# The low halves of the weights: from a subtraction on VectorE or GpSimd to a negating copy on ScalarE and an adding transfer

## The chip, the cores and the metric

The kernel runs on one core of a Trainium2 chip. The metric is the device time of one execution in microseconds (us). The kernel before takes 1946.34 us (median of 3 runs, 1944.94 to 1948.01).

The core has a matrix engine (TensorE: PE for the matmuls, PEld for the loads of their stationary operand), three engines for elementwise work (VectorE: DVE; ScalarE: ACT; GpSimd: POOL) and a queue for loads and stores (SyncE: SP). Each engine works through its own instructions in order; an instruction that waits for a semaphore holds up all behind it on that engine. Transfers can be issued from SP, ACT and POOL.

## The reference

One layer of a streaming encoder, applied to 1024 + 32 rows of width 1024, all in float32:

- an input layer norm;
- `x = LN1(alpha*x + 1/2*g1*SwiGLU_1(mod1(x)))`, with `SwiGLU(h) = (silu(h @ w1) * (h @ w3)) @ w2` and an inner width of 2816;
- `x = LN2(alpha*x + g2 * W_out[RG-LRU ; spatial gating](mod2(x)))`, a mixing stage with a recurrent and a gated branch of width 512 each;
- `x = LN3(alpha*x + 1/2*g3*SwiGLU_2(mod3(x)))`.

`mod_k(x) = x*(1 + scale_k(c)) + shift_k(c)` and `g_k = 1 + gate_k(c)`, where the nine vectors of length 1024 are `silu(c) @ w_ada + b_ada`, for two conditions c (one for the 1024 rows, one for the 32).

## The kernel before

**Precision.** TensorE works on `float32r`, a rounded float32. Each float32 operand is therefore kept as two parts, the rounded value `h` and the remainder `l = x - h`, and each product is three matmuls: `Wh*Xh + Wh*Xl + Wl*Xh`. `split` (L208) makes the parts: ACT copies the source into `h` (L209), and DVE, or another engine that is named, subtracts `h` from the source into `l` (L210).

**Weights.** All weights of the two feed-forward stages and of the mixing stage come as 156 raw tiles of 128x1024 float32 (512 KB), loaded by SP in a fixed order into 5 buffers (`w_raw`, L204). They are used as 440 halves of 128x512. `w_split` (L248) makes the next half of that order: it takes a tile from a ring of 8 buffers (tag `wh`; 12 halves have another home, `wx` or `tx`), finds its source (`w_source`, L229) and splits it. `w_get` (L261) hands a half to the matmuls; `w_rel` (L269) is called when a half has been used, splits as many further halves as the ring then has room for, and loads raw tiles ahead.

**Which engine subtracts.** `w_split` sends the subtraction to POOL where an engine is given, in the "window" around LN1 (`self.window`), and for the halves S1 to S4; otherwise to DVE. Six halves in `ffn_first` are given POOL by name.

**The fast tiles.** From column tile 9 of the first feed-forward stage on, and 3 of the second (32 tiles in all), w1 and w3 of a tile are treated as a 2x2 block matrix with a product of seven multiplications for two of the three row chunks. Such a tile has eight halves: A11, A21, A22, S2, A12, S1, S3, S4. The S halves are sums that POOL forms in place in the raw tiles: A21 -= A11 (L239), then A22 -= A21 (L241), which gives S2, then A11 += A22 (L243) for S1 and A12 -= A22 (L245) for S4; S3 is the changed A21. An in-place sum has to wait until everything that reads the raw tile has read it. `H_fast` (L852) multiplies them in the order A11, A21, S2, A12, S1, S3, A22, S4 and calls `w_rel` after each. `F` (L1006) then multiplies the gated result `g` by w2, for blocks of mostly two tiles; it uses four halves for two tiles.

**Beside it.** In the first feed-forward stage DVE also computes seven of the nine conditioning vectors (`ada_rest`, L685): 56 raw tiles `araw` (L693), in the same 5 buffers as the weights, are multiplied and summed (L759, L761); 14 times the sums go through TensorE to a row (L710), from POOL's queue to DRAM (L711) and back, turned (L716, two transfers), and are used by DVE (L721). POOL also forms block sums of x there (L818, L819) and, in the norms, an inverse square root (L562).

**What sets the order.** TensorE's instructions run in the order of the program. For the other engines a planner orders them: it goes by program order and priorities, and by when it reckons each instruction ready, from modelled durations. `startup` and `ffn_first` are the exception: there ACT, DVE and POOL keep the order that is written. Tile by tile the framework puts in all semaphore waits, a wait for a transfer's landing included.

Of the kernel before, what the change touches and what calls it, by code (L numbers as in the profile page):

```python
# [12 lines left out]
F32 = mybir.dt.float32  # L13
F32R = mybir.dt.float32r
AF = mybir.ActivationFunctionType
ALU = mybir.AluOpType
# [90 lines left out]
def raws_of(e):  # L107

    nm, t, h = e
    return [(nm, t)] if h in (0, 1) else [(f"{nm}w1", t), (f"{nm}w3", t)]  # L110
# [13 lines left out]
class Core:  # L124
# [123 lines left out]
    def w_split(self, e=None):  # L248
        n = self.n_split
        if n >= len(self.order):  # L250
            return
        it = self.order[n]
        e = e or (self.nc.gpsimd if self.window or str(it[2])[0] == "S" else None)
        while not all(r in self.raws for r in raws_of(it)):
            self.w_raw()
        w = self.w_tile(it)
        self.split(w[:, 0, :], w[:, 1, :], self.w_source(it), e)
        self.ws[it] = w
        self.n_split += 1

# [114 lines left out]
    def startup(self):  # L375
        nc, V, S = self.nc, self.nc.vector, self.nc.scalar
        sp, es = self.pool("start", side="right")
        self.ada_hl = []
        self.n_ada = 0
        self.ada_rw = []  # L380
        xt = []
        for i in range(9):
            if i < 8:
                t = sp.tile([P, D], F32, name=f"xt{i}")
                for h in range(2 if i == 0 else 1):
                    cs = slice(h * 512, (h + 1) * 512) if i == 0 else slice(0, D)
                    nc.sync.dma_start(t[:, cs], self.i["x"][i * P:i * P + P, cs])
            else:
                t = self.apool.tile([P, 4, 384], F32, tag="t4", name="xt8", bufs=2).rearrange("p a b -> p (a b)")[:, 0:D]
                nc.sync.dma_start(t[:NS], self.i["x"][NP:T])  # L390
            xt.append(t)

        self.nat = 4
        self.ada_nat = []
        for f in range(self.nat):
            w = [self.wpool.tile([P, 1024], F32, tag="wh", name="wnat", bufs=RING) for _ in range(2)]
            for j in range(2):
                nc.sync.dma_start(w[j], self.i["ada0"][2 * f + j].rearrange("p k c -> p (k c)"))
            self.ada_nat.append(w)
            if f == min(1, self.nat - 1):  # L400
                self.w_raw()
                self.w_raw()
        self.n_ada = 2 * self.nat
        self.ada_rw = [None] * self.n_ada
        self.ada_hl = [None] * self.n_ada

        for v in range(2):
            S.activation(self.cs[:, :, v], self.v("c", v * 8, v * 8 + 8), AF.Silu)
        self.split(self.c4[:, :, 0:2], self.c4[:, :, 2:4], self.cs)
        mv = sp.tile([P, 9, 2], F32, name="mv")  # L410
        rs = sp.tile([P, 9, 2], F32, name="rs")

        def stats(i):
            n = P if i < 8 else NS
            bs = sp.tile([P, 2, 6], F32, tag="bs", name="bs", bufs=2)
            for h in range(2):
                V.bn_stats(bs[:n, h, :], xt[i][:n, h * 512:(h + 1) * 512])
            V.bn_aggr(mv[:n, i, :], bs[:n])
            self.rsqrt(rs[:n, i, 0:1], mv[:n, i, 1:2])

        def norm(i):
            n = P if i < 8 else NS
            if i in (5, 8):
                V.tensor_scalar(xt[i][:n], xt[i][:n], mv[:n, i, 0:1], rs[:n, i, 0:1], ALU.subtract, ALU.mult)
                return
            V.scalar_tensor_tensor(rs[:n, i, 1:2], mv[:n, i, 0:1], -1.0, rs[:n, i, 0:1], ALU.mult, ALU.mult)
            S.activation(xt[i][:n], xt[i][:n], AF.Identity, scale=rs[:n, i, 0:1], bias=rs[:n, i, 1:2])

        banks = {}

        def turn(i):

            m = P if i < 8 else NS
            banks[i] = [self.ps() for _ in range(2)]
            for k in range(K):
                o = (k % 4) * P
                nc.tensor.transpose(banks[i][k // 4][:, o:o + m], xt[i][:m, k * P:(k + 1) * P], self.idn[:m, :m])
                self.pe += 0.213

        def out(i, dve):  # L440
            c, j = divmod(i, 3)
            m = P if i < 8 else NS
            for h in range(2):
                d = self.xacc[c][:, 4 * h:4 * h + 4, j * P:j * P + m]
                r = banks[i][h].rearrange("p (k t) -> p k t", k=4)[:, :, :m]
                if dve:
                    V.tensor_copy(d, r)
                else:
                    S.activation(d, r, AF.Copy)

        self.rows = {}
        for i in range(11):
            if i < 9:
                stats(i)
            if 0 < i < 10:
                norm(i - 1)
                turn(i - 1)
            if i == 9:
                self.ada_mm(0)
            if i > 1:  # L460
                out(i - 2, i > 7)
        for h in range(2):
            self.w_split()
        es.close()

    def ada_raw(self, n):
# [1156 lines left out]
```

## Time and profile before

| | before |
|---|---|
| median of 3 runs | 1946.34 us (1944.94 to 1948.01) |
| profiled execution: time | 1944.43 us |
| profiled execution: span of the instructions | 1942.7 us |
| granted TensorE clock, mean | 0.983 |
| PE / DVE / ACT / POOL busy | 1870.9 / 1291.3 / 696.4 / 483.2 us |
| transfers issued from POOL's queue | 42, none above 4 KB |

"Busy" counts the instructions that compute. A row of a list of groups reads: line, engine, operation, what it writes and reads, shape, count, then total busy us and mean ns of one, then the idle time of the engine before them and what ended most of it. A row of a table of stages reads: from and to in us, length, then for each engine the busy time and in brackets the number of instructions, then the granted clock, the busy share of the 16 transfer engines and the rate. A row of a timeline reads: start, duration, engine, line, operation, and in brackets how long the engine idled before it and which instruction released it.

The stages: start and first conditioning to 85 us; first feed-forward stage to about 820 us, with `ada_rest` beside it until about 608 us; LN1, mixing and LN2 to about 1215 us; the second feed-forward stage to about 1882 us; then the last norm.

### The profile page before, as it was taken

How to read it: one execution, taken by the hardware profiler on the slowest of the kernel's cores; microseconds unless marked ns; L12 is line 12 of the kernel's file. 1: busy time of each engine (PE TensorE's matmuls, PEld its weight loads, DVE VectorE, ACT ScalarE, POOL GpSimd, SP SyncE). 2: the span in 40 equal slices, each digit the busy share in tenths (PEclk: the TensorE clock that was granted, in tenths of full speed). 3: DMA queues.
4: the chain of work that ended last, by engine and by line, in shares of the span. 5: the costliest groups of instructions: out<-in, count | busy, mean ns of one | idle time of the engine just before them, and what ended most of it. 6: DMA issues, size and time to landing. Idle time of an engine off the chain costs nothing.

```text
span 1942.7 us, 28443 instructions
## 1 busy us (share of the span) xinstructions
PE 1870.9 (96%) x11434; PEld 1820.6 (94%) x11434; DVE 1291.3 (66%) x2296; ACT 696.4 (36%) x1228; POOL 483.2 (25%) x398
## 2 busy tenths in 40 slices
PE   6999999989998999989999999999999999999996
PEld 3899999889898999989979999999999999999996
DVE  7855678898877645683776558875545554555477
ACT  5552122232332232336553517522332233223324
POOL 2201160234333333222000000042334233323410
PEclk9999999999998999989989999999999999999998
DMA  7332333132331111122011311102120111011102
GB/s 275 125 115 77 110 103 121 59 104 93 98 127 37 44 66 44 55 87 93 28 33 51 133 55 44 44 23 65 45 65 22 58 53 64 24 53 57 44 1 90
DMA packets 40500, 140.16 MB, mean 72 GB/s; under 512 B 5652, under 2 KB 8340, under 8 KB 39600
## 3 DMA queue, kind: packets, MB, share of 16 engines
q1 hardware_dynamic: 37104, 128.98, 19.6%
q10 hardware_dynamic: 1920, 9.24, 1.2%
q0 software_dynamic: 1344, 0.12, 0.4%
q8 instruction: 90, 1.47, 0.3%
q14 instruction: 42, 0.34, 0.1%
HBM read 129.53 MB, written 8.79 MB: 71 GB/s over the span
## 4 chain that ended last, share of the span: by engine, by line
PE 81%; DVE 10%; ACT 3%; issue 2%; DMA 2%; POOL 2%; SPq 0%; POOLq 0%; DVEq 0%; ACTq 0%
PE ps L152 78%; DVE acc L761 1%; PE psl L152 1%; DVE xl L548 1%; DVE wh L210 1%; DMA mod<-mrow 1%; PE psa L152 1%; PE psz L152 1%; PE psm L152 1%; DMA araw<-ada 1%; DVE s L674 0%; PE psg L152 0%; ACT t L538 0%; POOL s L818 0%; DVE tot L980 0%
## 5 line engine op out<-in xcount | busy, mean ns | idle before, releaser
L152 PE MATMUL ps<-xh,wh 128*128 128x384 f32 (+1 forms) x4016 | 953.7, 320 | 6.9 <-ACT s L874 5.0
L152 PEld LDWEIGHTS ps<-xh,wh 128*128 128x128 f32 x4016 | 698.9, 189 | 12.2 <-ACT s L874 5.7
L152 PE MATMUL ps<-xl,wh 128*128 128x384 f32 (+1 forms) x2008 | 641.7, 320 | 3.3 <-DVE xl L548 3.2
L152 PE MATMUL ps<-g,wh 128*128 128x384 f32 (+1 forms) x2808 | 474.8, 328 | 17.0 <-DVE s L674 7.1
L152 PEld LDWEIGHTS ps<-g,wh 128*128 128x128 f32 x2808 | 461.3, 191 | 26.8 <-DVE s L674 8.4
L209 ACT ACTIVATE wh<-raw 128x512 fp32r<-128x512 f32 x428 | 266.2, 628 | 524.9 <-PE ps L152 436.8
L152 PEld LDWEIGHTS ps<-xl,wh 128*128 128x128 f32 x2008 | 378.6, 189 | 7.1 <-DVE xl L548 5.3
L210 DVE TENSOR_TENSOR wh<-raw,wh 128x512 fp32r<-128x512 f32 x283 | 204.6, 729 | 246.0 <-ACT wh L209 244.6
L210 POOL TENSOR_TENSOR wh<-raw,wh 128x512 fp32r<-128x512 f32 x145 | 208.8, 1442 | 321.8 <-ACT wh L209 321.5
L974 DVE SCALAR_TENSOR_TENSOR xb<-ps,gt,xb 128x384 f32<-128x384 f32 (+1 forms) x352 | 151.9, 486 | 87.4 <-PE ps L152 71.1
L761 DVE SCALAR_TENSOR_TENSOR acc<-araw,cs,acc 128x512 f32<-128x512 f32 x196 | 154.1, 825 | 15.3 <-DMA araw<-ada 15.1
L152 PE MATMUL ps<-tx,wh 128*128 128x384 f32 x768 | 138.9, 336 | 0.1
L974 DVE SCALAR_TENSOR_TENSOR xa<-ps,gt,xa 128x384 f32<-128x384 f32 (+2 forms) x288 | 122.7, 483 | 22.8 <-PE ps L152 22.8
L152 PEld LDWEIGHTS ps<-tx,wh 128*128 128x128 f32 x768 | 132.5, 188 | 0.6 <-DVE s L867 0.4
L239 POOL TENSOR_TENSOR raw<-raw 128x512 f32<-128x512 f32 x32 | 46.3, 1448 | 324.0 <-DVE wh L210 324.0
L209 ACT ACTIVATE g<-s 128x384 fp32r<-128x384 f32 (+1 forms) x126 | 60.7, 492 | 138.7 <-DVE s L674 138.7
L210 DVE TENSOR_TENSOR g<-s,g 128x384 fp32r<-128x384 f32 (+1 forms) x126 | 84.9, 683 | 23.6 <-ACT g L209 22.5
L867 DVE TENSOR_TENSOR s<-s,ps 128x384 f32<-128x384 f32 x128 | 70.5, 551 | 37.4 <-PE ps L152 37.3
L562 POOL TENSOR_TENSOR r<-r,half 128x3 f32<-128x3 f32 x8 | 7.4, 923 | 310.2 <-DVE r L561 310.2
L669 ACT ACTIVATE s<-ps 128x384 f32<-128x384 f32 (+1 forms) x100 | 44.9, 452 | 99.4 <-PE ps L152 99.1
L152 PE MATMUL ps<-T,wh 128*128 128x384 f32 x384 | 72.9, 337 | 0.0
L152 PEld LDWEIGHTS ps<-T,wh 128*128 128x128 f32 x384 | 67.9, 188 | 0.4 <-issue 0.2
(237 smaller groups left out, 1694.6 us busy)
## 6 DMA issues: line engine op xcount, KB each, us to landing
raw<-wst SPq DMA_DIRECT2D x156, 512.0 KB, 3.3
araw<-ada SPq DMA_DIRECT2D x56, 512.0 KB, 3.3
wnat<-ada SPq DMA_DIRECT2D x8, 512.0 KB, 9.9
raw<-ada SPq DMA_DIRECT2D x8, 512.0 KB, 3.7
xt<-x SPq DMA_DIRECT2D x7, 512.0 KB, 7.7
sp<-xa ACTq DMA_DIRECT2D x2, 1536.0 KB, 5.8
xb<-sp ACTq DMA_DIRECT2D x2, 1536.0 KB, 9.4
y<-xb SPq DMA_DIRECT2D x4, 768.0 KB, 3.3
```

Source lines behind the costliest of these rows:

```text
L152: self.nc.tensor.matmul(out, a, b, start=start, stop=stop, skip_group_check=True)
L209: self.nc.scalar.activation(dst_h, src, AF.Copy)
L210: (e or self.nc.vector).tensor_tensor(dst_l, src, dst_h.bitcast(F32), ALU.subtract)
L239: G.tensor_tensor(a["A21"], a["A11"], a["A21"], ALU.subtract)
L548: V.tensor_tensor(xl, tmp, xh.bitcast(F32), ALU.subtract)
L562: self.nc.gpsimd.tensor_tensor(out, out, self.half[:n, :w], ALU.pow)
L669: self.nc.scalar.activation(s, x[:, :n], AF.Silu)
L761: V.scalar_tensor_tensor(acc[:, v, :], r[:, kk, :], self.cs[:, k, v:v + 1], acc[:, v, :], ALU.mult, ALU.add)
L867: V.tensor_tensor(out, x, ps[:, :n], ALU.add)
L974: V.scalar_tensor_tensor(X[:, m, a + o:a + o + w], ps[:, o:o + w], self.gt[:, s, m, v:v + 1], X[:, m, a + o:a + o + w], ALU.mult, ALU.add)
```

## The change

`w_split` splits a half in the old way only where an engine is given or in the window. Every other half is made so: ACT copies the source into the first part, ACT copies that first part with a factor of -1 into the second part, and a transfer issued from POOL's queue adds the raw source to the second part. The S halves take this way too; before, POOL subtracted them. The two halves at the end of `startup`, which had no engine given and so went to DVE, are now given DVE by name.

```diff
@@ -250,11 +250,18 @@
         if n >= len(self.order):
             return
         it = self.order[n]
-        e = e or (self.nc.gpsimd if self.window or str(it[2])[0] == "S" else None)
+        e = e or (self.nc.gpsimd if self.window else None)
         while not all(r in self.raws for r in raws_of(it)):
             self.w_raw()
         w = self.w_tile(it)
-        self.split(w[:, 0, :], w[:, 1, :], self.w_source(it), e)
+        src = self.w_source(it)
+        if e:
+            self.split(w[:, 0, :], w[:, 1, :], src, e)
+        else:
+
+            self.nc.scalar.activation(w[:, 0, :], src, AF.Copy)
+            self.nc.scalar.activation(w[:, 1, :], w[:, 0, :].bitcast(F32), AF.Copy, scale=-1.0)
+            self.nc.gpsimd.dma_start(w[:, 1, :], src, accum_op=ALU.add)
         self.ws[it] = w
         self.n_split += 1
 
@@ -460,7 +467,7 @@
             if i > 1:
                 out(i - 2, i > 7)
         for h in range(2):
-            self.w_split()
+            self.w_split(V)
         es.close()
```

## The prediction

> **What bounds the kernel now.** I read the page's first block and the groups of line 209 and 210, then the stages, then who waits for whom in the first feed-forward stage.
>
> ```profile
> span 1942.7 us, 28443 instructions
> ...
> PE 1870.9 (96%) x11434; PEld 1820.6 (94%) x11434; DVE 1291.3 (66%) x2296; ACT 696.4 (36%) x1228; POOL 483.2 (25%) x398
> ...
> L209 ACT ACTIVATE wh<-raw 128x512 fp32r<-128x512 f32 x428 | 266.2, 628 | 524.9 <-PE ps L152 436.8
> ...
> L210 DVE TENSOR_TENSOR wh<-raw,wh 128x512 fp32r<-128x512 f32 x283 | 204.6, 729 | 246.0 <-ACT wh L209 244.6
> L210 POOL TENSOR_TENSOR wh<-raw,wh 128x512 fp32r<-128x512 f32 x145 | 208.8, 1442 | 321.8 <-ACT wh L209 321.5
> ```
>
> TensorE is busy 96% of the span. The 428 copies of L209 mostly wait for TensorE to give a ring buffer back, so the weights run as far ahead as the ring allows. The stages say where TensorE is not full:
>
> ```profile
> core 0: us, PE busy (x) PEld busy (x) DVE busy (x) ACT busy (x) POOL busy (x), PEclk, DMA share, GB/s
> 85.00:370.00 285.00, 279.09 (x1699) 272.47 (x1697) 195.14 (x334) 82.25 (x158) 58.67 (x57) 0.99 0.32 104
> 370.00:608.00 238.00, 222.24 (x1313) 214.17 (x1314) 207.91 (x351) 71.54 (x135) 82.60 (x68) 0.96 0.29 94
> 608.00:820.00 212.00, 212.00 (x1316) 212.00 (x1316) 124.39 (x244) 63.40 (x120) 73.60 (x56) 1.00 0.16 53
> 820.00:1058.00 238.00, 225.94 (x1284) 210.09 (x1284) 161.45 (x273) 117.56 (x189) 29.55 (x34) 0.96 0.17 60
> 1058.00:1215.00 157.00, 157.00 (x973) 155.77 (x972) 102.81 (x153) 78.43 (x114) 2.56 (x3) 1.00 0.21 72
> 1215.00:1882.00 667.00, 667.00 (x4176) 666.87 (x4174) 389.29 (x716) 212.28 (x403) 209.48 (x152) 1.00 0.14 45
> ```
>
> From 608 to 820 and from 1058 to 1882 us (1036 us together) TensorE never idles: nothing done to the weights can gain there, it can only lose. TensorE idles 285.00 - 279.09 = 5.9 us from 85 to 370, 15.8 us from 370 to 608 and 12.1 us in LN1 and the mixing. In the second of these DVE is busy 207.91 of 238 us (87%), against 68% in the first. Who waits there (85 to 608 us):
>
> ```profile
> PEld ps L152 <- DVE s L674: 8.4, 4, 3.3
> PEld ps L152 <- ACT g L209: 5.8, 4, 2.2
> ...
> DVE wh L210 <- ACT wh L209: 31.7, 18, 5.1
> DVE mod L721 <- DMA mod<-mrow: 25.9, 8, 4.6
> ...
> DVE acc L761 <- DMA araw<-ada: 15.1, 9, 3.4
> ```
>
> TensorE waits for the gating that DVE has not come to (L674) and for what follows from it, and DVE in turn sits 31.7 us in front of subtractions whose first part isn't there yet.
>
> **The change part by part.** *How many.* There are 440 halves: 428 of tile wh, 12 with another home. The old way stays for 2 in startup, 6 with POOL by name, and 13 of the window (of POOL's 145, 128 are the four S halves of 32 tiles and 6 are named; that leaves 11, and 2 in the other home). So 440 - 2 - 6 - 13 = 419 take the new way; of these POOL subtracted 128 and DVE 291.
>
> *DVE* loses 291 x 0.729 = 212 us. What of it lies where TensorE waits:
>
> ```profile
> 85.00:370.00 285.00, 274.56 (x1669) 270.37 (x1667) 34.72 (x46) 28.97 (x47) 1.13 (x1) 0.99 0.32 104
> 370.00:608.00 238.00, 218.15 (x1287) 212.18 (x1288) 30.13 (x37) 38.41 (x62) 35.77 (x26) 0.96 0.29 94
> ...
> 1215.00:1882.00 667.00, 653.54 (x4090) 652.84 (x4088) 82.18 (x119) 122.48 (x195) 108.65 (x76) 1.00 0.14 45
> ```
>
> These are the same stages for the instructions on weight tiles alone, with L209 and L210 on DVE, ACT and POOL. From 370 to 608 us DVE sheds 30.1 us and falls from 87% to 75%. Between the two stages the idle share of TensorE goes with DVE's: 2.1% (5.9 of 285) at 68%, 6.6% (15.8 of 238) at 87%, a slope of 0.24 points a point. At 75% that is 3.6%, or 8.5 us, a gain of some 7 us. From 85 to 370 DVE falls to 56%, for which the line gives no idling; I take half of the 5.9 us, 3 us. Bounds: no gain, and all 21.7 us plus what the clock of 0.96 and 0.99 costs (0.04 x 238 + 0.01 x 285 = 12 us).
>
> *ACT* gets 419 x 0.628 = 263 us more, 36% to about 50%. In the full stages that is at most 195 x 0.628 = 122 us on top of 212 in 667 us. In the written order at the end of `ffn_first` the last negating copy stands before the first gating:
>
> ```profile
> 84.63 0.63 ACT L209 ACTIVATE wh<-raw 128x512 fp32r<-128x512 f32 x1 [1.34 <-PE ps L152]
> 85.17 0.47 ACT L669 ACTIVATE s<-ps 128x384 f32<-128x384 f32 x1
> ```
>
> The first row, the last of those copies, follows a wait for TensorE that takes up what came before, so only its own second copy is exposed: 0.6 us of loss.
>
> *POOL* sheds 128 x 1.44 = 184 us and gets 419 transfers. A POOL transfer of this shape is not in the trace. The nearest:
>
> ```profile
> L711 POOL DMA_DIRECT2D mrow<-row x14: 534/544/716, 128.8 to 609.2; - x14
> L716 POOL DMA_DIRECT2D mod<-mrow x28: 747/760/814, 131.1 to 614.3; - x28
> ...
> raw<-wst SPq DMA_DIRECT2D x156, 512.0 KB, 3.3
> ...
> xb<-sp ACTq DMA_DIRECT2D x2, 1536.0 KB, 9.4
> ...
> mod<-mrow POOLq DMA_DIRECT2D x28, 2.0 KB, 2.9
> ...
> mrow<-row POOLq DMA_DIRECT2D x14, 4.0 KB, 1.6
> ```
>
> Issuing costs POOL 0.54 to 0.76 us; I take 0.76, 318 us in all, which it has idle. Landing: 1.6 us at the least, 9.4 at the most. The transfer moves 256 KB, half of a raw load, but must read its destination too, so I take the raw load's 3.3 us. The Trainium skill, "DMA: Bandwidth & Descriptors", section on the anatomy of one DMA, gives about 2.0 us plus the bytes at 436 GB/s, an estimate of 2.6 us for 256 KB; its rules for authors add that an accumulate reads its destination and writes it later. For a raw load its formula gives 3.2 us, and this trace has 3.3. With 2.6 the lateness of 4.0 us that follows, and with it the second rival's price, would be 3.3 us.
>
> *Is a half still there in time?* A part that came 0.73 us after the first copy now comes after 0.63 + 0.76 + 3.3 = 4.7 us: 4.0 us later. The longest chain is that of S2, which needs the whole of A22 first, since the in-place sum may not overwrite a raw tile that a transfer still reads:
>
> ```profile
> 1362.01 0.63 ACT L209 ACTIVATE wh<-raw 128x512 fp32r<-128x512 f32 x1 [1.46 <-PE ps L152]
> ...
> 1363.58 1.29 POOL L241 TENSOR_TENSOR raw<-raw 128x512 f32<-128x512 f32 x1 [0.94 <-DVE wh L210]
> ...
> 1365.92 0.63 ACT L209 ACTIVATE wh<-raw 128x512 fp32r<-128x512 f32 x1
> ...
> 1380.88 0.63 ACT L209 ACTIVATE wh<-raw 128x512 fp32r<-128x512 f32 x1 [0.97 <-PE ps L152]
> ```
>
> The first row is A22's copy, the third S2's; the fourth is released by the end of A21's matmuls in the next tile, which is where S2's begin. New: 1362.01 + 1.26 + 0.76 + 3.3 = 1367.3, sum to 1368.6, two copies to 1369.9, transfer to 1373.9. TensorE needs it at 1380.9, so 6.9 us are left, and a landing may take 3.3 + 6.9/2 = 6.8 us before TensorE waits. In the ring as a whole a half has some eight halves of matmuls between its turn and its use. Hence no loss in the full stages. If the cover went, each microsecond of landing above 6.8 would cost 2 us a tile, 64 us in all.
>
> *Raw tiles* come free later by the same 4.0 us. That delays loads of `araw`, for which DVE waits; this I enter with 2 us of loss, between none and the rival below.
>
> *Sum.* 1944.43 - 7 - 3 + 0.6 + 2 = 1937 us, made against the profiled execution's own time (its span of 1942.7 us and 1.7 us around it). The median of the runs is 1.9 us above that time, so the sum stands for some 1939 us of a run; I take **1938 us**, -0.4%, since the clock's part is left out of the sum. A difference of 0.2% (3.9 us) is about what a measurement of this kernel can tell from no change.
>
> **The rivals.**
>
> *ScalarE's line (slower).* At the end of a block of tiles the planner put S2's copy ahead of the silu that the last gating needs (L916), although the copy waits for POOL's sum:
>
> ```profile
> 1331.01 1.37 POOL L241 TENSOR_TENSOR raw<-raw 128x512 f32<-128x512 f32 x1 [2.37 <-DVE wh L210]
> 1331.20 5.96 PE L152 MATMUL ps<-g,wh 128*128 128x384 f32 x36
> ...
> 1332.42 0.63 ACT L209 ACTIVATE wh<-raw 128x512 fp32r<-128x512 f32 x1 [1.95 <-POOL raw L241]
> ...
> 1332.96 0.51 ACT L916 ACTIVATE s<-s 128x384 f32<-128x384 f32 x1
> ...
> 1334.77 0.97 DVE L210 TENSOR_TENSOR g<-s,g 128x384 fp32r<-128x384 f32 x1 [0.59 <-ACT g L209]
> ```
>
> The low part of g ends at 1335.74, and TensorE wants it with the last 6 of the 36 matmuls, about 1336.1: 0.4 us to spare. If the order stays, the sum comes 4.0 us later and the second copy 0.6 after it, so that TensorE waits 4.2 us. With 15 such block ends that is 63 us less the forecast's gain: about 2002 us. For it: the order that is there now. Against it: a planner that reckons with a transfer in the chain sees S2 ready after the silu and puts it behind. It decides at about 0.4 us of lateness.
>
> *Late conditioning (slower).* SP's loads of `araw` wait for weight tiles:
>
> ```profile
> SPq L693 <- DVE wh L210: 83.2, 18, 11.8
> ```
>
> Each of the 18 comes 4.0 us later, up to 72 us of waiting in DVE's line, and POOL's transfers L711 and L716 stand behind weight transfers that wait for ACT. If half of it reaches TensorE, 36 us against the 10 gained: about 1972 us. Against it: DVE sheds 65 us of work there and 31.7 us of waits.
>
> *No change.* TensorE's stalls before 608 us come from the returns of the conditioning rows (25.9 us of DVE waiting at L721) and not from DVE's load; then the relief buys nothing: 1946 us.
>
> *POOL held by its transfers (slower).* A second transfer of L716 starts 3.8 us after the first, with POOL idle between:
>
> ```profile
> 131.06 0.81 POOL L716 DMA_DIRECT2D mod<-mrow  x1 [1.51 <-DMA mrow<-row]
> 134.86 0.76 POOL L716 DMA_DIRECT2D mod<-mrow  x1 [2.99 <-issue]
> ```
>
> If every weight transfer held POOL that long, 195 halves from 1215 to 1882 us would take 741 us beside 101 us of POOL's other work, in 667 us: 175 us of loss there, some 235 in all, about 2180 us. Against it: L716 moves single elements, 128 x 4 runs of 4 bytes, where a weight transfer has 128 runs of 2 KB.
>
> *It doesn't do what it says:* the subtraction could stay where it was only if an engine were given everywhere, which the diff excludes.
>
> **How the numbers follow.** Forecast 0.45, no change 0.20, late conditioning 0.17, ScalarE's line 0.12, POOL held 0.06. The forecast's own range is 1928 to 1942 us. The range for 8 times in 10 leaves out ScalarE's line and POOL held (0.18) and reaches from 1925, where most of the 21.7 us is won, to 1990. Of the forecast 0.43 lies beyond 0.2%. Faster 0.43, same 0.22, slower 0.35.
>
> **What would show it.** Right: 419 transfers of 256 KB on POOL's queue, landing in under 6.8 us; from 608 to 820 and 1058 to 1882 TensorE still full; DVE some 30 us less busy from 370 to 608, and TensorE idle 9 us there and not 16. Wrong: TensorE waiting at the start of w2 blocks for g (ScalarE's line); longer waits of DVE for `araw` or at L721; POOL idle "issue" time before weight transfers; a landing far above 3.3 us, which would break the cover of S2 and with it the forecast.

## The result, and the profile after

The changed kernel takes 1995.31 us (median of 4 runs, 1992.95 to 1998.74) against 1945.64 us of the kernel before beside it: a ratio of 1.0258 (95% interval 1.0236 to 1.028), 2.6% slower. The forecast was 1938 us, with a range of 1925 to 1990 us: the wrong direction, and the time lies outside the range. The profiled execution took 1998.74 us, with a mean granted clock of 0.975 (before 0.983).

First the page after: its first rows, then groups of the halves and their transfers.

```profile
span 1997.0 us, 29461 instructions
...
PE 1883.0 (94%) x11434; PEld 1830.1 (92%) x11434; DVE 1046.6 (52%) x2005; ACT 935.3 (47%) x1647; POOL 659.7 (33%) x689
...
L264 POOL DMA_DIRECT2D wh<-raw x409 | 358.7, 887 | 682.0 <-ACT wh L263 364.3
...
L262 ACT ACTIVATE wh<-raw 128x512 fp32r<-128x512 f32 x409 | 254.1, 625 | 470.2 <-PE ps L152 254.5
...
L263 ACT ACTIVATE wh<-wh 128x512 fp32r<-128x512 f32 x409 | 255.8, 629 | 10.0
...
L239 POOL TENSOR_TENSOR raw<-raw 128x512 f32<-128x512 f32 x32 | 43.4, 1358 | 144.7 <-DMA wh<-raw 117.9
```

(Lines behind `w_split` stand 7 lower now: L669 became L676, and so on.) The change does what it says: 409 of 419 halves are of tile wh, ACT makes both copies in 0.63 us each, and the transfer's issue costs POOL 0.887 us. DVE sheds 244.7 us (1291.3 to 1046.6): the 212 us of the subtractions, and the rest because other work of it ran shorter, such as the low parts of `g` (126 of them took 84.9 us before and 67.6 after; why isn't shown). TensorE's idle time grows all the same, from 71.8 to 114.0 us, and its busy time by 12.1 us for the same 11434 matmuls, with a mean granted clock of 0.975 in place of 0.983. The table of stages, first in stretches that the prediction used, then in two of the second feed-forward stage:

```profile
85.00:370.00 285.00, 274.82 (x1664) 269.75 (x1665) 154.00 (x273) 104.13 (x196) 91.07 (x100) 0.98 0.56 147
370.00:608.00 238.00, 207.04 (x1194) 198.60 (x1194) 155.22 (x291) 97.61 (x178) 92.17 (x94) 0.92 0.59 138
608.00:820.00 212.00, 201.75 (x1240) 199.95 (x1239) 87.28 (x208) 97.30 (x176) 91.00 (x93) 0.98 0.61 131
820.00:1058.00 238.00, 220.90 (x1248) 208.51 (x1247) 142.93 (x239) 121.68 (x203) 52.68 (x59) 0.96 0.33 89
...
1263.00:1880.00 617.00, 617.00 (x3877) 617.00 (x3877) 262.74 (x554) 300.97 (x555) 250.23 (x253) 1.00 0.59 124
1880.00:1935.00 55.00, 51.13 (x293) 50.26 (x292) 20.72 (x39) 24.93 (x48) 20.57 (x22) 0.97 0.54 104
```

From 370 to 608 us DVE is busy 155.22 of 238 us (65%, before 87%), and TensorE idles 31.0 us in place of 15.8, at a clock of 0.92 in place of 0.96. The second feed-forward stage is full, as before, but for its end, which comes some 50 us later than before: from 1880 to 1935 us TensorE idles 3.9 us. Most of the loss lies in the first stage: LN1's first inverse root, on POOL, comes 48.0 us later. Of these, some 10 us are there by 378 us of the time before (a row's copy, L710 before and L717 after, matched one by one), 43 by 593 us (the silu of L916, now L923); then nothing is added until 806 us, and the last 5 at the stage's end. The loss is made from 378 to 600 us above all, where the fast tiles run beside the conditioning. The lateness stays at 48 us up to 1843 us of the time before, and is 54 us from 1859 on. The inverse root's row in the timeline before (L562), then after (L569):

```profile
834.17 1.12 POOL L562 TENSOR_TENSOR r<-r,half 128x3 f32<-128x3 f32 x1 [41.34 <-DVE r L561]
```

```profile
882.20 1.13 POOL L569 TENSOR_TENSOR r<-r,half 128x3 f32<-128x3 f32 x1
```

Who waits for whom from 85 to 860 us, before and then after (sum in us, times, longest):

```profile
POOL raw L239 <- DVE wh L210: 115.3, 13, 14.6
...
DVE mod L721 <- DMA mod<-mrow: 29.1, 9, 4.6
...
ACT wh L209 <- POOL raw L241: 15.2, 8, 3.0
DVE acc L761 <- DMA araw<-ada: 15.1, 9, 3.4
```

```profile
DVE acc L768 <- DMA araw<-ada: 59.3, 15, 9.1
ACT wh L262 <- POOL raw L241: 59.1, 11, 9.5
DVE mod L728 <- DMA mod<-mrow: 51.8, 13, 10.7
...
POOL raw L239 <- DMA wh<-raw: 45.2, 11, 7.0
```

Four waits go with it. POOL's in-place sums (L239) stand until a transfer has read the raw tile; S2's copy on ACT stands behind the sum of L241; DVE waits for the conditioning's raw tiles (four times as long as before) and for its returning rows. POOL idled in front of L239 before as well, and longer, for VectorE's subtractions (115.3 us): that wait alone proves nothing, and what counts is that the sum now comes so late that ACT waits for it, 59.1 us in place of 15.2. One such chain, from the timelines of POOL, ACT, DVE and PE after:

```profile
461.55 1.29 POOL L239 TENSOR_TENSOR raw<-raw 128x512 f32<-128x512 f32 x1 [6.12 <-DMA wh<-raw]
...
466.10 1.25 POOL L241 TENSOR_TENSOR raw<-raw 128x512 f32<-128x512 f32 x1 [2.46 <-DMA wh<-raw]
...
467.39 0.63 ACT L262 ACTIVATE wh<-raw 128x512 fp32r<-128x512 f32 x1 [5.69 <-POOL raw L241]
467.92 0.61 ACT L209 ACTIVATE acchl<-acc 128x512 fp32r<-128x512 f32 x1
...
468.57 0.69 DVE L210 TENSOR_TENSOR acchl<-acc,acchl 128x512 fp32r<-128x512 f32 x1 [5.32 <-ACT acchl L209]
469.18 0.61 DVE L981 SCALAR_TENSOR_TENSOR xa<-ps,gt,xa 128x384 f32<-128x384 f32 x1
...
469.85 1.33 PE L152 MATMUL ps<-g,wh 128*128 128x384 f32 x3 [3.69 <-DVE xa L981]
```

The sum of L239 waits 6.12 us for a transfer, that of L241 2.46 us for the next one; ACT stands 5.69 us; behind its copy stands the copy of `acchl`, DVE waits for that, its gated sum L981, which gives a PSUM buffer back, comes late, and TensorE idles 3.69 us. TensorE waited for no weight here: everything in this chain is work that stood behind a weight in an engine's line.

The 6 us at the end of the second stage have such a chain too, from one timeline of all engines:

```profile
1896.88 1.28 POOL L239 TENSOR_TENSOR raw<-raw 128x512 f32<-128x512 f32 x1 [5.24 <-DMA wh<-raw]
...
1899.53 0.63 ACT L262 ACTIVATE wh<-raw 128x512 fp32r<-128x512 f32 x1 [8.32 <-POOL raw L241]
...
1900.73 0.47 ACT L904 ACTIVATE s<-ps 128x384 f32<-128x384 f32 x1
...
1901.25 0.44 PE L152 MATMUL ps<-xh,wh 128*128 128x384 f32 x1 [2.62 <-ACT s L904]
```

ACT stands 8.32 us in front of S2's copy, the silu of L904 comes behind both copies, and TensorE waits 2.62 us for that silu.

### The profile page after: what moved, and what is told of

Its sections match the earlier page's. It is cut to its first block, busy times and chain, and to the rows that moved or that the text cites. A ratio compares the mean times of both kernels' runs of the same rounds, so it can differ in the third digit from the quotient of the medians.

```text
span 1997.0 us, 29461 instructions
## 1 busy us (share of the span) xinstructions
PE 1883.0 (94%) x11434; PEld 1830.1 (92%) x11434; DVE 1046.6 (52%) x2005; ACT 935.3 (47%) x1647; POOL 659.7 (33%) x689
## 3 DMA queue, kind: packets, MB, share of 16 engines
q0 software_dynamic: 61680, 109.98, 31.3%
## 5 line engine op out<-in xcount | busy, mean ns | idle before, releaser
L264 POOL DMA_DIRECT2D wh<-raw x409 | 358.7, 887 | 682.0 <-ACT wh L263 364.3
L262 ACT ACTIVATE wh<-raw 128x512 fp32r<-128x512 f32 x409 | 254.1, 625 | 470.2 <-PE ps L152 254.5
L263 ACT ACTIVATE wh<-wh 128x512 fp32r<-128x512 f32 x409 | 255.8, 629 | 10.0
L981 DVE SCALAR_TENSOR_TENSOR xb<-ps,gt,xb 128x384 f32<-128x384 f32 (+1 forms) x352 | 152.8, 488 | 119.8 <-PE ps L152 98.4
L768 DVE SCALAR_TENSOR_TENSOR acc<-araw,cs,acc 128x512 f32<-128x512 f32 x196 | 147.5, 800 | 59.3 <-DMA araw<-ada 59.3
L152 PE MATMUL ps<-tx,wh 128*128 128x384 f32 x768 | 144.9, 345 | 18.0 <-DVE s L874 18.0
L152 PEld LDWEIGHTS ps<-tx,wh 128*128 128x128 f32 x768 | 137.4, 194 | 19.1 <-DVE s L874 19.0
L981 DVE SCALAR_TENSOR_TENSOR xa<-ps,gt,xa 128x384 f32<-128x384 f32 (+2 forms) x288 | 123.5, 486 | 37.2 <-PE ps L152 36.6
L239 POOL TENSOR_TENSOR raw<-raw 128x512 f32<-128x512 f32 x32 | 43.4, 1358 | 144.7 <-DMA wh<-raw 117.9
L210 DVE TENSOR_TENSOR g<-s,g 128x384 fp32r<-128x384 f32 (+1 forms) x126 | 67.6, 542 | 36.4 <-ACT g L209 35.4
L676 ACT ACTIVATE s<-ps 128x384 f32<-128x384 f32 (+1 forms) x100 | 44.0, 450 | 71.2 <-PE ps L152 70.9
L681 DVE TENSOR_TENSOR s<-s 128x384 f32<-128x384 f32 x64 | 35.8, 560 | 59.1 <-ACT s L923 58.1
```

Source lines behind the costliest of these rows:

```text
L152: self.nc.tensor.matmul(out, a, b, start=start, stop=stop, skip_group_check=True)
L210: (e or self.nc.vector).tensor_tensor(dst_l, src, dst_h.bitcast(F32), ALU.subtract)
L239: G.tensor_tensor(a["A21"], a["A11"], a["A21"], ALU.subtract)
L262: self.nc.scalar.activation(w[:, 0, :], src, AF.Copy)
L263: self.nc.scalar.activation(w[:, 1, :], w[:, 0, :].bitcast(F32), AF.Copy, scale=-1.0)
L264: self.nc.gpsimd.dma_start(w[:, 1, :], src, accum_op=ALU.add)
```

## The experiments

Each is the changed kernel with the edit shown, unless it says otherwise; ratios are to the kernel before, in runs beside it on the same chip. A ratio's 0.1% is 1.95 us.

**Where: one stage at a time.** Two runs, with the old way in the first feed-forward stage alone (the condition `== "f1"`), and everywhere but there (`!=`):

```diff
+        if not e and it[0][:2] == "f1":
+            e = self.nc.gpsimd if str(it[2])[0] == "S" else self.nc.vector
```

> The changed kernel with the old subtraction for every half of the first feed-forward stage (the S halves on GpSimd, the others on VectorE), the new way for the mixing and the second stage only. Theory A (ScalarE's line: in-place sums that wait for landings, and what stands behind them on ScalarE, cost time only where VectorE also carries the conditioning, in the first stage): within 8 us of the kernel before, 1940 to 1954 us, the 160 to 170 transfers left cost nothing up to 1880 us. Theory B (late conditioning rows and raw tiles): the same, since the rows are all in the first stage. Rival C (the transfers and the 5% more work cost everywhere, clock included): half of the loss stays, some 1970 us.

> The changed kernel with the new way in the first feed-forward stage only, the old subtraction in the mixing and the second stage. Theories A and B: about 42 to 48 us above the kernel before, 1988 to 1994 us. Rival C (a cost everywhere): about half, 1970 us. With the run that keeps the first stage old, the two losses should add up to the whole one of 50 us.

With the first stage old: 1951.54 us, ratio 1.0037 (1.0025 to 1.005). With the new way in the first stage only: 1993.53 us, 1.0259 (1.0242 to 1.0276). The first stage alone gives a loss as large as the whole. The rest alone costs some 7 us (0.37%), and its trace shows a loss in one place, the end of the second stage: TensorE idles 5.3 us between 1263 and 1880 us, nearly all of them after 1763. Added up, the two give 2.96% against 2.58% for the whole; the difference of 0.38% is about the noise of such a sum (0.3%). Rival C, a cost everywhere, is out.

**What the relief is worth: the second copy without its transfer.**

```diff
-            self.nc.gpsimd.dma_start(w[:, 1, :], src, accum_op=ALU.add)
```

> The changed kernel with the negating copy but without the adding transfer: the second part stays the negated first part, so the weight is left out of the product. ScalarE has all its added work and GpSimd none. Theories A and B (the landing is what costs): the loss is gone and VectorE's relief shows, 1930 to 1945 us. Rival D (ScalarE's 263 us of added copies in front of its gating work are the cost): 1970 us or above.

Measured: 1919.86 us, 0.9879 (0.9858 to 0.9899), 1.2% faster than before. It is faster than either theory had it, and the near-zero products might have done that, through the clock. So the same was run with the second copy scaled by 0:

```diff
-            self.nc.scalar.activation(w[:, 1, :], w[:, 0, :].bitcast(F32), AF.Copy, scale=-1.0)
-            self.nc.gpsimd.dma_start(w[:, 1, :], src, accum_op=ALU.add)
+            self.nc.scalar.activation(w[:, 1, :], w[:, 0, :].bitcast(F32), AF.Copy, scale=0.0)
```

> The run without transfer again, with the second copy scaled by 0 in place of -1: the second part is zero and not the negated first part, so TensorE multiplies numbers of the usual size, and only the low part of these weights is left out. If the 24 us of that run were VectorE's relief: again 1915 to 1925 us. If they came from the near-zero products (a clock of 1.00 in the first stage where the kernel before has 0.94 to 0.99): 1930 to 1945 us.

Measured: 1920.87 us, 0.9881 (0.9867 to 0.9896). The data play no part. The stages of this run:

```profile
85.00:370.00 285.00, 280.98 (x1715) 274.40 (x1713) 166.66 (x291) 112.26 (x212) 55.97 (x58) 1.00 0.32 104
370.00:608.00 238.00, 231.73 (x1424) 226.31 (x1425) 176.32 (x353) 114.89 (x205) 50.85 (x48) 0.99 0.30 98
```

TensorE idles 10.3 us from 85 to 608 us (before 21.7) and the clock is 1.00 and 0.99 (before 0.99 and 0.96). ScalarE's 409 added copies cost nothing that shows, rival D is out, and leaving the subtractions out is worth 1.19%, 23 us. Three things are in that: the relief of VectorE, GpSimd's S subtractions gone, and raw tiles that are free after ScalarE's first copy, where before they were held until the subtraction. SyncE's loads of `araw` wait 59.8 us for weight work in this run and 93.1 before (83.2 for VectorE, 9.9 for GpSimd). The three were not tested apart. The transfer then costs 1.0258 - 0.9881 = 3.77%, 73 us.

**Whether the in-place sums' waits are it: A11, A21, A12, A22 old.** The first experiment's edit with the condition `str(it[2])[0] == "A"`.

> The changed kernel with the old subtraction on VectorE for A11, A21, A12 and A22, everywhere; the four S halves and all whole halves keep the new way. The in-place sums of GpSimd then wait for VectorE as before, and not for a landing, while a raw tile is still held until the landing of S3 and S4. Theory A (ScalarE's line behind the sums): the loss falls from 50 to about 10 us, 1950 to 1962 us, and ScalarE's waits for the sum of L241 fall from 169.5 to below 60 us. Theory B (raw tiles held longer, transfers of the rows behind weight transfers): 25 us of the loss or more stay, 1970 us or above.

Measured: 1968.3 us, 1.0126 (1.0111 to 1.0141). The waits from 85 to 860 us:

```profile
DVE acc L770 <- DMA araw<-ada: 54.9, 15, 9.0
...
ACT wh L264 <- POOL raw L241: 13.1, 8, 2.3
```

ScalarE's wait for the sum falls back to 13.1 us (over the whole run to 31.3, expected below 60), and half of the loss with it. The other half stays, just under what theory B had named, and with it VectorE's wait for `araw`. Theory A is half of the story at most: with the waits of the sums the edit also takes away 128 of the transfers, and what they load on the transfer engines.

**The whole halves alone in the new way.** The same edit with `str(it[2])[0] in "AS"`, so that nothing of a fast tile takes a transfer.

> The changed kernel with the old subtraction for the eight halves of every fast tile (A on VectorE, S on GpSimd); the new way stays for the whole halves (w1, w3 of the plain tiles, w2, the mixing). No in-place sum waits for a landing. Theory A alone: the loss up to 378 us stays at about 10 us, and 5 more at the end, 1950 to 1962 us. Theory B1 (raw tiles of w2 held beside the loads of the conditioning weights): between 1955 and 1968 us, the value of the run with only A11, A21, A12, A22 old. If only the S halves' landing mattered there, this run comes to 1944 us or below.

Measured: 1964.57 us, 1.0106 (1.0084 to 1.0129). So 21 us are lost although no in-place sum waits for a landing; DVE's wait for `araw` is 44.0 us there (15.1 before). A11, A21, A12 and A22 cost another 1.32% (1.0258 - 1.0126); the S halves show nothing beyond the noise (1.0126 against 1.0106).

**Hold, traffic, queue: a transfer that reads something else, or less.** The transfer adds the first part itself in place of the raw half, so that the raw tile is free after ScalarE's first copy:

```diff
-            self.nc.gpsimd.dma_start(w[:, 1, :], src, accum_op=ALU.add)
+            self.nc.gpsimd.dma_start(w[:, 1, :], w[:, 0, :].bitcast(F32), accum_op=ALU.add)
```

> The changed kernel with the transfer adding the first part (tile wh itself) in place of the raw half: as many bytes, the same queue and the same wait of TensorE for it, but the raw tile is free after ScalarE's first copy and no in-place sum waits for a landing. The second part comes out as zero, so the low part of these weights is left out. Theory A+B1 (the loss is what stands behind a raw tile that is held until the landing: the in-place sums and the loads of new raw tiles): within 10 us of the run without transfer (1920 us). Rival B2 (the transfers' traffic and their queue, in which the conditioning rows stand): 1950 us or above. Half and half would come out near 1940 us.

Measured: 1956.04 us, 1.0065 (1.0039 to 1.009): above the half and half of the expectation, so traffic and queue are a cause of their own. Next, 16 columns of the raw half:

```diff
+            self.nc.gpsimd.dma_start(w[:, 1, 0:16], src[:, 0:16], accum_op=ALU.add)
```

> The changed kernel with a transfer of 16 of the 512 columns (8 KB in place of 256 KB); the other columns of the second part stay the negated first part. Issue, queue and most of the landing stay, the traffic is nearly gone. Theory B2 (traffic): close to the run without transfer, 1920 to 1935 us. Theory A+B1 (the lateness behind a held raw tile): by landing in proportion; with a landing of 2 to 3 us in place of 4.0, some 1.5 us less of 4.8 us lateness, so 1965 to 1985 us if the loss goes with the lateness, and 1950 us if only what goes beyond a slack of some 2 us counts.

> The run with the transfer of 16 columns, with the second copy scaled by 0: those 16 columns of the second part are the raw weights, the others zero. The difference to the zero run without transfer is the price of a transfer of 8 KB, with its issue, its landing of some 2.1 us and the raw tile held until then, and nearly no traffic: 27 us if the data play no part, as between the two runs with the scale of -1.

Measured: 1947.48 us, 1.0008 (0.9995 to 1.0021) with the scale of -1, and 1948.36 us, 1.0014 (1.0003 to 1.0025) with 0. The data again play no part. And last, 16 columns of the first part, with the scale of 0:

```diff
+            self.nc.gpsimd.dma_start(w[:, 1, 0:16], w[:, 0, 0:16].bitcast(F32), accum_op=ALU.add)
```

> The changed kernel with the second copy scaled by 0 and a transfer that adds 16 columns of the first part: neither the raw tile is held nor is there traffic to speak of; 409 issues on GpSimd (0.9 us each), their landing, and the wait of the weights for it stay. Those 16 columns of the second part are the first part once more, the others zero. If the hold alone makes the 27 us of the run with 16 raw columns: 1920 to 1928 us. If it is the queue (the rows behind the transfers, GpSimd's issue time) or the weights' own lateness: 1940 us or above. Then the hold would have cost little by itself.

Measured: 1933.67 us, 0.9936 (0.9918 to 0.9954), between the two expectations. The four make a table, as ratios:

| | raw tile free after the first copy | raw tile held until the landing |
|---|---|---|
| 8 KB | 0.9936 | 1.0014 |
| 256 KB | 1.0065 | 1.0258 |

No transfer at all is 0.9881. Issue, queue and the weights' own lateness cost 0.55% (11 us, give or take 5), the traffic, with the longer landing that comes with it, 1.29% (25, give or take 6), and the hold 0.78% (15, give or take 4) where a landing takes 2.1 us, but 1.93% (38, give or take 7) where it takes 4.0. The give and take come from the two intervals, as the root of the sum of their squares. Hold and traffic make each other dearer: beside the hold, the traffic costs 2.44% (47 us), so the sum 11 + 25 + 38 is one way of sharing out the 73 us, not the only one.

Two cautions. The "hold" here is counted from a raw tile that is free after the first copy. The kernel before held its tiles until the subtraction, so against that kernel it costs less than 38 us. The 23 us gained without a transfer contain what the earlier release brought there; so long as the relief itself cost nothing, at least some 15 (38 - 23) are left. And the planner's order isn't quite the same either: of the instructions up to 900 us, matched between the traces of the two 8 KB runs, 13 of 539 on ACT, 30 of 1033 on DVE and 14 of 156 on POOL stand elsewhere, so a part of what is called the hold may be that. The 8 KB run without the hold and the run without transfer have the same order.

The waits from 85 to 860 us go the same way. First 8 KB with the hold, then 8 KB without, then 256 KB without:

```profile
DVE acc L768 <- DMA araw<-ada: 46.8, 15, 7.1
DVE mod L728 <- DMA mod<-mrow: 41.1, 11, 7.6
...
ACT wh L262 <- POOL raw L241: 24.0, 11, 5.7
```

```profile
DVE mod L728 <- DMA mod<-mrow: 44.8, 12, 6.9
...
DVE acc L768 <- DMA araw<-ada: 23.1, 14, 3.7
...
ACT wh L262 <- POOL raw L241: 5.8, 5, 3.3
```

```profile
DVE mod L728 <- DMA mod<-mrow: 57.5, 13, 8.9
...
DVE acc L768 <- DMA araw<-ada: 33.3, 14, 4.2
...
ACT wh L262 <- POOL raw L241: 4.5, 5, 2.0
```

In the first and the second of these, SyncE's loads of `araw` wait for the weights' tiles, first until a transfer has landed, then until ScalarE has copied:

```profile
SPq L700 <- DMA wh<-raw: 89.0, 18, 10.6
```

```profile
SPq L700 <- ACT wh L262: 61.0, 16, 17.1
```

The hold is seen there and in the waits for `araw` and for the sum of L241 (46.8 and 24.0 against 23.1 and 5.8 us), the traffic in those for `araw` and the rows (33.3 and 57.5 against 23.1 and 44.8).

**The rows' queue.** The transfers of the conditioning rows are issued from ScalarE, in the changed kernel and, as the control, in the kernel before:

```diff
-            nc.gpsimd.dma_start(d, row)
+            nc.scalar.dma_start(d, row)
...
-                    nc.gpsimd.dma_start(self.mod[:, m, 4 * h:4 * h + 4, v],
+                    nc.scalar.dma_start(self.mod[:, m, 4 * h:4 * h + 4, v],
```

> The changed kernel with the transfers of the conditioning rows (mrow<-row and mod<-mrow) issued from ScalarE's queue in place of GpSimd's, away from the weight transfers. If the rows' place behind the weight transfers on GpSimd's queue is a cause of its own (VectorE waits 51.8 us for mod): 1975 us or below. If the rows are late for the traffic and the held raw tiles: 1985 us or above.

> The kernel before with the same change of queue for the conditioning rows, as the control: between 1930 and 1950 us. Below 1940 us would say that GpSimd's own work already held up the rows, so that the same gain in the changed kernel proves nothing of the weight transfers.

Measured: the changed kernel 1977.02 us, 1.0174 (1.0148 to 1.02), 0.84% below what it was; the kernel before **1935.1 us, 0.9951** (0.9934 to 0.9967), 0.49% below. In the changed kernel VectorE's wait for the rows is nearly gone, while those for `araw` and for the sum stay:

```profile
ACT wh L262 <- POOL raw L241: 68.6, 12, 8.1
DVE acc L768 <- DMA araw<-ada: 60.2, 16, 13.3
...
DVE mod L728 <- DMA mod<-mrow: 10.4, 5, 5.2
```

The changed kernel lies between its two bounds, the control below its 1940 us. Both edits gain, and the gains differ by 0.35% (7 us, give or take 7): issuing the rows from GpSimd cost time before the change as well, and what the weight transfers add to that is small and not settled. The control is the only kernel here that computes the whole reference and beats the kernel before. The Trainium skill, "DMA: Bandwidth & Descriptors", section "Issuing engines are not separate DMA queues", says that issuing from several engines saves only the time it takes to issue. Here the 42 issues took 28 us of GpSimd's busy time (483.2 to 455.1 us), and moving them was worth 10 us of the kernel's time, though GpSimd is busy only a quarter of it. The edit does more than save that time: an issue on GpSimd stands in line behind whatever GpSimd waits for, and a returning row lands in 2.3 us from ScalarE's queue in place of 2.9. Which of these the 10 us are is not shown.

The same two edits on the kernel whose transfer adds the first part itself:

> The changed kernel with the transfer adding the first part itself (full traffic, no raw tile held, second part zero) and the rows' transfers on ScalarE's queue. If the 36 us of the run with full traffic and no hold come from the rows behind the transfers on GpSimd's queue: 1925 us or below. If they come from the traffic (loads of 4.3 us in place of 3.3): 1942 us or above, no more than the control's 10 us below 1956.

Measured: 1942.22 us, 0.9981 (0.9968 to 0.9995), 0.84% below the same without the queue's edit. Neither bound settles it alone: the number is that of the second reading, but it came by 0.84% (16 us) and not by the control's 10. What is left above the run without any transfer, 1.0%, has neither the hold nor the rows' queue in it: it is traffic, with GpSimd's 419 issues and the weights' own lateness.

**Relief by GpSimd in place of a transfer.** The kernel before, with GpSimd subtracting for the whole halves of the first stage:

```diff
-        e = e or (self.nc.gpsimd if self.window or str(it[2])[0] == "S" else None)
+        e = e or (self.nc.gpsimd if self.window or str(it[2])[0] == "S" or (it[0][:2] == "f1" and it[2] in (0, 1)) else None)
```

> The kernel before with GpSimd instead of VectorE subtracting for the whole halves of the first feed-forward stage (w1, w3, w2; 1.44 us in place of 0.73 each, no transfer, no second copy). If VectorE's relief is what the run without transfer gained its 24 us by, and 0.7 us of lateness is harmless, this gains as well: 1925 to 1940 us. If GpSimd's in-place sums and the S halves now stand behind these subtractions, 1950 us or above.

Measured: 1961.68 us, 1.0091 (1.0071 to 1.0111): slower, though VectorE sheds work and there is no transfer. Its waits for `araw` grow as well, and SyncE's loads of `araw` (L693) now wait for GpSimd to be done with a raw tile, 106.8 us in all and up to 19.6 at a time (before 9.9 for GpSimd and 83.2 for VectorE, 93.1 together, and up to 11.8 at a time):

```profile
DVE acc L761 <- DMA araw<-ada: 39.5, 15, 6.7
```

```profile
SPq L693 <- POOL wh L210: 106.8, 20, 19.6
```

This looks like the hold once more, by another hand: GpSimd comes to its subtraction late. That the hold is what these 17 us are was not tested, and it also shows that relief of VectorE by itself need not gain.

What wasn't tried: more buffers for the raw tiles, which would test the hold directly.

## Why the prediction was wrong, point by point

- **Halves (419: 128 from POOL, 291 from DVE).** Held: 409 of tile wh, and 8 and 2 in the other homes.
- **ACT, 0.63 us for a copy, 263 us in all.** Held (L263: 255.8 us for 409), with no cost that shows in the run without transfer.
- **POOL's issue at 0.76 us.** 0.887 us, a term slightly small.
- **Landing of 3.3 us, lateness of 4.0 us.** The landing's median is 4.0 us; 0.63 + 0.89 + 4.0 - 0.73 makes a lateness of 4.8. That is below the 6.8 us that the cover of S2 allowed, but 40 of the 419 took longer, up to 16.1 us. The formula of the Trainium skill ("DMA: Bandwidth & Descriptors", section on the anatomy of one DMA), which is given there for transfers issued from GpSimd, gave an estimate of 2.6 us; the runs agree with it for 8 KB (2.1 us measured) and not for 256 KB that are added to their destination.
- **No loss in the full stages.** Held from 600 to 806 us of the time before, by the matched silus, and from 1263 to 1880 us, where ScalarE waits for the sum as well (169.5 us over the whole run, 59.1 of them before 860) and TensorE does not. It failed at the end of the second stage, where 6 us are lost behind a sum that came late. The ring covers the weights nearly everywhere, as reckoned, even with landings above 6.8 us (TensorE waited 5.5 us for landings in the whole run, 0.2 of them in the second stage).
- **DVE's relief, 7 + 3 us.** Too small for what leaving the subtractions out gains: 23 us without the transfer, the upper bound of 21.7 us of idle time and some of the clock's part. How much of that is DVE's relief, and how much raw tiles that come free earlier, is open.
- **Raw tiles come free later, 2 us of loss.** This is the step that failed. The hold cost 38 us beside the full traffic, counted from a tile that is free after the first copy, and at least some 15 against the kernel before (the planner's slightly different order included). It was priced as a load that comes 4.0 us later into DVE's slack; but a held raw tile stops three lines at once: SP's loads of `araw` (96.4 us of waiting for landings in the changed kernel), POOL's in-place sums, and behind those ACT's copies (59.1 us) with the conditioning's and the gating's work in its line. The sum had followed the sums' delay (the S2 chain) only as far as the weights.
- **The transfers' traffic and line: not in the sum at all.** The 419 transfers were costed as issue and landing. Their load on the transfer engines (25 us, the longer landing included, and 47 beside the hold) and the place of the rows in the line behind them (within the 11 us of issue and queue) had no term; that the rows stand behind weight transfers was named in a rival alone.
- **0.6 us at startup.** TensorE waits 2.26 us for the silu (L676) at 86.16 us; small either way.
- **Rivals.** Late conditioning had the mechanism and the place (chance 0.17; 36 us for the loads alone, and 1972 us), ScalarE's line had the wait but mostly the wrong place: of the block ends of the second stage only the last lost time, 6 us and not 63; in the first stage the four A halves cost 26 us net of their relief, traffic included. The two were priced as alternatives, and they came together: 23 us gained, 73 lost. No change and POOL held by its transfers are out (POOL idled 49.6 us with no wait shown before 60 of the transfers, far from 3.8 us before each).
- **The argument from the slope** (TensorE's idle share against DVE's busy share) gave a gain of the right sign for what leaving the subtractions out is worth, and was blind to what it is paid with: after the change DVE is busy 65% from 370 to 608 us and TensorE idles twice as long.

## What to carry to other kernels

A transfer that takes over an engine's step keeps its source until it lands; list everybody who waits for that source (the next load into the buffer, in-place work, and all that stands behind these on their engines), not only who waits for the result. A ring that runs ahead hides a late result but not a late release of something shared. And price a transfer three ways: landing, the share of the transfer engines, and who stands behind its issue on that engine.

## What the runs showed of the hardware

Transfers from 85 to 860 us in the changed kernel, by queue (packets, MB, share of the 16 engines), and by kind (KB, median us to landing):

```profile
q0 software_dynamic: 26784, 46.46, 34.6%
q1 hardware_dynamic: 16867, 61.43, 24.4%
...
wh<-raw POOLq DMA_DIRECT2D x173, 256.0 KB, 4.0
raw<-wst SPq DMA_DIRECT2D x62, 512.0 KB, 4.1
araw<-ada SPq DMA_DIRECT2D x56, 512.0 KB, 4.0
```

An adding transfer took 34.6 / 46.46 = 0.74% of the engines' time for a MB, a plain load 24.4 / 61.43 = 0.40%: nearly twice as much, so that 256 KB added weigh about what 512 KB loaded do. (The rows' small transfers are in the 34.6; they were 0.9 before.) The transfers of 8 KB, in runs of 64 bytes, still took 6.5%. The engines are busy 0.56 to 0.61 of the time in the first stage (0.16 to 0.32 before), far from full, and the loads still land in 4.0 to 4.1 us in place of 3.3. And from 370 to 608 us the granted clock is lower where TensorE idles more: 0.92 with 31.0 us idle in the changed kernel, 0.96 with 15.8 before, 0.99 with 6.3 in the run without transfer.
